# A hybrid decoder block: the merge of the attention groups stores its weights in natural token order and multiplies in halves

## The chip, the cores and the metric

The kernel runs on one core of a Trainium2 chip. The metric is the device time of one execution in microseconds (us), of which several runs are taken and the median is given. The trace is one execution, taken by the hardware profiler.

## What is computed

The block has two branches over 1024 tokens of width 1024: a gated delta rule (8 heads) and a dilated sliding-window attention (4 heads). The change lies in the attention. Each of its heads has three groups with dilations 1, 4 and 16. A group gives, for every token, an unnormalised numerator of 128 channels, the softmax's denominator and the maximum of the row. The groups are then merged by weights that come from the maxima and the denominators:

```
def _dilated_attention(q, k, v):
    ...
    parts = [_dilated_group(q[:, :, i], k[:, :, i], v[:, :, i], win, dil, slopes[i])
             for i, (win, dil) in enumerate(DIL_GROUPS)]
    m_all = parts[0][2]
    for _, _, mx in parts[1:]:
        m_all = jnp.maximum(m_all, mx)
    num = 0.0
    den = 0.0
    for nm, dn, mx in parts:
        sc = jnp.exp(mx - m_all)
        num = num + nm * sc[..., None]
        den = den + dn * sc
    return (num / den[..., None]).reshape(Bn, Sn, DIL_W)
...
        o_b = _dilated_attention(q_b, k_b, v_b) * jax.nn.silu(z_b.astype(f32))
```

## The kernel before

The input projections are done in *units*: two blocks of 128 output columns times 1024 tokens, as a Strassen product of seven products with 12 matmuls each (`gemm_steps`, line 113; the matmuls are line 189). A stationary block is split in two parts, `wh` by ScalarE (line 139) and `wl` by VectorE (line 140), one product ahead of its use; the sums of the stationary blocks are made by GpSimd (lines 152, 153, 165, 166). Results are added from PSUM by VectorE (lines 130, 199, 212).

A head of the attention has five units (`att_unit`, line 753), and its three groups run beside the later ones (`attention`, line 550): scores (line 578), a combined subtraction and minimum on VectorE (line 582), an exponential on ScalarE (line 584), a transpose (line 591), a copy (line 593) and the weighted sum (line 601). A group keeps its tokens in the order (residue, position): group 1 by residues of 4, group 2 by residues of 16. The numerators `num` are `[128 channels, 1024 tokens]` in that order.

The order of TensorE is written out by hand: every generator gets *positions* on a scale in which one unit is 1.0 (`add_stream`, `spread`, and the tables from line 802 on), and `emit` takes the steps in order of position. For the other engines and the DMA queue the Tile scheduler sets the order at build time: of the instructions that its model holds to be ready, the one traced first goes first. Each engine then works strictly in that order. All DMAs are issued from SP, also in order.

`merge` (line 612) is a generator with positions of its own, `MERGE` (line 803), counted from the first unit of its head. At 6.07 the statistics of the three groups are transposed, stored to scratch memory and loaded as `[64, 16]` tiles with 16 tokens to a partition; at 6.52 the weights are worked out (lines 634 to 644) and stored to scratch `w_d`, each group in its own order; from 7.104 on they are loaded broadcast to 128 partitions, multiplied into the numerators (line 654), and the numerators are summed (line 658). The natural order of the tokens comes with these sums: the first group's numerator is viewed with steps of 4 and 16 elements. The last step multiplies by the gate `zs` and stores the head's output.

```
        w_d = dr.tile([3, S], F32, name="w_d", tag="w_d", bufs=2)
        nc.sync.dma_start(w_d[0].rearrange("(l r) -> l r", r=16), cm[:, 0, 0])
        nc.sync.dma_start(w_d[1].rearrange("(r l s) -> l r s", r=4, s=4),
                          cm[:, 0, 1].rearrange("p (r s) -> p r s", s=4))
        nc.sync.dma_start(w_d[2].rearrange("(r l) -> l r", r=16), cm[:, 0, 2])
        yield
        for g in range(3):
            wb = ap_.tile([128, S], F32, name="wb", bufs=2)
            nc.sync.dma_start(wb, w_d[g:g + 1, :].to_broadcast([128, S]))
            V.tensor_tensor(nums[g], nums[g], wb, OP.mult)
            yield
```

The rows of the three stores are 64 B (line 646), 16 B (line 647) and 4 B (line 649) long. After a head's merge the next head's first group runs beside the same unit; after the last head (positions 22 and on) the convolutions of the delta rule (line 904) and its preparation (transposes in line 948) follow. The buffers of the delta rule are taken from the memory of the attention's pool, tile by tile as that comes free.

Of the kernel before, what the change touches and what calls it, by code (L numbers as in the profile page):

```python
# [9 lines left out]
F32 = mybir.dt.float32  # L10
F32R = mybir.dt.float32r
AF = mybir.ActivationFunctionType
OP = mybir.AluOpType
# [3 lines left out]
S = 1024  # L17
# [14 lines left out]
def hybrid_block(ctx: ExitStack, tc: tile.TileContext, x, norm_w, w_in, conv_w, a_log, dt_bias,  # L32
# [27 lines left out]
    @contextmanager  # L60
    def band(level):
        """Instructions traced inside come before all of a higher level when both are ready."""
        saved = tc.cur_priority
        tc.cur_priority = marks.get(level, level * 1000000)
        yield
        marks[level] = tc.cur_priority
        tc.cur_priority = saved

    @contextmanager
    def later(n):  # L70
        """As if traced n instructions later."""
        saved = tc.cur_priority
        tc.cur_priority = saved + n
        yield
        tc.cur_priority = saved
# [24 lines left out]
    ORDER = (("a", "A11", "B11"), ("b", "S2", "T2"), ("a", "A12", "B21"), ("b", "S3", "T3"),  # L100
             ("c", "S1", "T1"), ("b", "A22", "T4"), ("c", "S4", "B22"))
    # the same where the sums of the stationary blocks come late
    ORDER_LATE = (ORDER[0], ("o", "A12", "B21")) + (ORDER[1],) + ORDER[3:]
    # and those of the moving blocks too
    ORDER_LEAD = (ORDER[0], ORDER[2]) + (ORDER[4], ORDER[1], ORDER[3]) + ORDER[5:]

    last_add = [None]
# [5 lines left out]
    def gemm_steps(ops, raw, nk, dest, after, mid=None, late=False, third=None, ahead=0, lead=None):  # L113
        """raw(cb, khalf) -> [128, kh, 128] float32 of column block cb (overwritten).
        dest(cb, half) -> (output AP, view of a [128, 512] result with the output's shape);
        the view of block 0 is the identity or that of block 1. mid() may add to the
        incomplete result of block 1, half 0. With ahead the stationary blocks are made ready one
        product ahead, and the steps end after every three products of one contraction block; lead (with a
        tile for T2, gets a function for the first stationary sum): the sums of either operand come late."""
# [12 lines left out]
        def split(v, first=False):  # L132
# [7 lines left out]
            i = eng.tensor_tensor(wl[:, :kh], v, wh[:, :kh].bitcast(F32), OP.subtract)  # L140
            if third and seen["b"] == 1:
                with tc.issue_after(i.ins):
                    third()
# [86 lines left out]
    def w_raw(w2d, c0, c1, nk, get=raw_tile, which=((0, 0), (1, 1), (1, 0), (0, 1)), tl=None):  # L230
        """Load the two column blocks; 2-D weight [K, N]."""
# [21 lines left out]
    # per head, [p, f] by chunk: exp(-|gc[f] - gc[p]|), and the same with zeros where f < p  # L253
# [5 lines left out]
    # raw weights of the first two units: what is used first beside the first half of the tokens  # L259
# [27 lines left out]
    # norm_w on all partitions  # L287
# [6 lines left out]
    # Moving operands of the Strassen products: sums of the normed rows (quarters of a tile of 128 tokens and  # L294
    # its partner 512 tokens on), transposed on chip and split in two float32r parts.
# [59 lines left out]
    def lead_stream(units):  # L355
        """The first two units; either half of the tokens as it comes."""
# [5 lines left out]
        # S3's slots hold the first stationary blocks  # L362
# [7 lines left out]
        def product(u, n=None):  # L370
            """The next product of unit u; beside it the operand n."""
            for i in range(4):
                next(g[u])
                if n:
                    for j in COLS[i]:
                        part_of_rows(n, j)
                yield
# [46 lines left out]
    # convolution weights and the inner norm's, by channel  # L424
# [6 lines left out]
    def beta_decay():  # L431
        # b and a: the two float32r parts of the 16 columns side by side as one stationary block;
        # second half of the tokens: A21 W0 + A22 W1 = S1 W0 + A22 (W1 - W0)
# [43 lines left out]
        # log1p(e) = ln(u) + (e - (u - 1)) / u, u = 1 + e  # L477
# [40 lines left out]
    def perm(g, ap):  # L518
        """View of [128, n] natural tokens in the group's order (residue, position)."""
# [3 lines left out]
    def proj_unit(b0, b1):  # L523
        """b = (column, dest(half) -> (out AP, psum view), after(half))."""
# [25 lines left out]
    def attention(g, hh, t, st, nums):  # L550
        """Three steps for each block of 128 queries, after two for the values."""
# [60 lines left out]
    def merge(hh, st, nums, t):  # L612
# [8 lines left out]
        # partition = token // 16; the second group's 16 residues are kept in the order (r, s) of 4 s + r  # L621
# [8 lines left out]
        def nat(v, g):  # L630
            """[64, 16] in the order (s, r)."""
# [10 lines left out]
        V.reciprocal(nm, nm)  # L642
        for g in range(3):
            V.tensor_tensor(nat(cm[:, 0, g], g), nat(nm, 0), nat(cm[:, 0, g], g), OP.mult)
        w_d = dr.tile([3, S], F32, name="w_d", tag="w_d", bufs=2)
        nc.sync.dma_start(w_d[0].rearrange("(l r) -> l r", r=16), cm[:, 0, 0])
        nc.sync.dma_start(w_d[1].rearrange("(r l s) -> l r s", r=4, s=4),
                          cm[:, 0, 1].rearrange("p (r s) -> p r s", s=4))
        nc.sync.dma_start(w_d[2].rearrange("(r l) -> l r", r=16), cm[:, 0, 2])
        yield  # L650
        for g in range(3):
            wb = ap_.tile([128, S], F32, name="wb", bufs=2)
            nc.sync.dma_start(wb, w_d[g:g + 1, :].to_broadcast([128, S]))
            V.tensor_tensor(nums[g], nums[g], wb, OP.mult)
            yield
        for g in (1, 2):
            d = DIL[g][1]
            V.tensor_tensor(nums[0].rearrange("p (l r) -> p r l", r=d),  # L658
                            nums[0].rearrange("p (l r) -> p r l", r=d),
                            nums[g].rearrange("p (r l) -> p r l", r=d), OP.add)  # L660
            yield
        V.tensor_tensor(zs[:, :S], zs[:, :S], nums[0], OP.mult)
        nc.sync.dma_start(oB_d[hh], zs[:, :S])
# [3 lines left out]
    def decays(h):  # L667
        """The decay matrices of a head of the gated delta rule, two chunks at a time."""
# [69 lines left out]
    def ya_pair(i):  # L738
        """Two blocks of the first branch's projection, times their gates."""
# [13 lines left out]
    def att_unit(hh, t, pair):  # L753
        """Units of a head, in order: q and k of the first group, v of the first and q of the second,
        k and v of the second, q and k of the third, z and v of the third."""
# [17 lines left out]
    def unit_stream(units):  # L773
        """28 steps each; the weights of the next unit are loaded and made ready beside one. A unit: the two
        blocks (column, dest(half) -> (out AP, psum view), after(half)), the weights, the moving operands."""
# [22 lines left out]
    # The order of the tensor engine, by positions: one unit of the projections in a step.  # L798
    # FIRST: the unit beside which the first convolutions of the gated delta rule run; step n of it has the
    # preparation of half n and the recurrence of half n - 1. RAW, SUMS: sub-steps of a unit. GATES: the gate  # L800
    # units before the end of the rule.
    ATT00, ATT0, ATT1, ATT2 = (2.2, 3.13), (2.139, 3.1), (3.042, 4.541), (5.111, 5.892)
    MERGE, DECAY = (6.07, 6.52, 7.104, 7.12, 7.372, 7.42, 7.584, 7.672, 7.72), (2.417, 2.2)
# [47 lines left out]
    # distances for the two banded groups (previous tile | own tile) and for the 2 x 64 blocks  # L851
# [12 lines left out]
    # rows of the second block do not see the keys of the first  # L864
# [13 lines left out]
    dn = ExitStack()  # L878
    dnp = dn.enter_context(tc.tile_pool(name="dn", bufs=1, reuse_waits="tile"))
    # wmask[j, m] = 1 where j lies in the first block of m's pair of blocks of 16  # L880
# [7 lines left out]
    # one matrix per chunk; a step of 2064 leads from one diagonal block to the next, over chunks too  # L888
# [23 lines left out]
    def scaled(e, o, i, col):  # L912
        """o[p, c, :] = i[p, c, :] * col[p, c]"""
# [6 lines left out]
    def dn_conv(h, hf, t, o):  # L920
        """After either tap of the three convolutions."""
# [7 lines left out]
    def dn_prep(h, hf, o):  # L929
# [59 lines left out]
        # inverse of I + am: 16 x 16 blocks by substitution, then doubled  # L989
# [18 lines left out]
    def dn_run(h, hf, o, state):  # L1008
# [9 lines left out]
        def second(m, b):  # L1018
            """Columns of the second block of each pair of blocks of b."""
# [21 lines left out]
        # blocks of 32: two pairs, 0 and 1, 2 and 3  # L1041
# [18 lines left out]
        # the last doubling acts on one block of 64 x 64  # L1060
# [12 lines left out]
        # recurrence over the four chunks  # L1073
# [64 lines left out]
    def steps(positions):  # L1138
        """Positions of the gated delta rule's steps on the scale of units: the first step takes two."""
# [16 lines left out]
    fin = ctx.enter_context(tc.tile_pool(name="fin", bufs=1, reuse_waits="tile"))  # L1156
    # either half of the contraction, [token block, contraction block, token]
# [5 lines left out]
    def stage(lo, hi, ops_d, kb):  # L1163
        """The sums of the Strassen operands for contraction blocks kb and kb + 4, after the loads."""
# [21 lines left out]
    def split_block(t, tags, eng=V):  # L1186
        """[128, 1024] as two float32r parts."""
# [7 lines left out]
    def sources(n, src, ops_d, t):  # L1195
        """The half t of operand n of a Strassen product; src(contraction block, column half)."""
# [4 lines left out]
    def operand(n, ops, place, tile_of, srcs_of, eng=lambda t: V):  # L1201
        """Operand n into its slots; srcs_of(n, t) None: tile_of(n, t) is loaded."""
# [18 lines left out]
    # the operands used first wait where the sum of the branches comes later  # L1221
# [6 lines left out]
    def stage_a(kb):  # L1228
        """The sums of the first branch's operands for contraction blocks kb and kb + 4, after the loads."""
# [15 lines left out]
    def operand_steps(n):  # L1245
        """Operand n of the projection of the first branch: the loads if it is not there, then its two halves."""
# [196 lines left out]
```

## Time and profile before

| | us |
|---|---|
| median of 3 runs | 1505.6 |
| lowest and highest run | 1503.93, 1506.83 |
| span of the profiled execution, first to last instruction | 1503.7 |
| TensorE busy | 1402.2 (93%) |
| VectorE busy | 1061.7 (71%) |
| ScalarE busy | 728.3 (48%) |
| GpSimd busy | 417.2 (28%) |

The profiled execution's own time is its span; what lies around the span is not in the trace, and the median of the runs is 1.9 us above it. In the rows PE is TensorE, PEld its weight loads, DVE VectorE, ACT ScalarE, POOL GpSimd and SPq the queue on which SP issues DMAs. A matmul's duration reaches past the start of the next one, since matmuls are pipelined: the distance of the starts is what counts. "Idle before" is the time for which the engine had nothing to do, with what ended it.

### The profile page before, as it was taken

To read this page: it belongs to the slowest core of one execution; us is meant where nothing else is said; L and a number is where in the kernel's file an instruction comes from. 1 tells how busy PE (TensorE), PEld (TensorE's weight loads), DVE (VectorE), ACT (ScalarE), POOL (GpSimd) and SP (SyncE) were. 2 spreads that over 40 slices of the span, in tenths; PEclk is the share of its full clock that TensorE was granted. 3 is DMA by queue.
4 is the path that set the end of the run, shared out by engine and by line. 5 is a ranking of instruction groups with operands and counts; after the bars stand their busy time and mean duration, and the time that the engine had idled before them with its cause. 6 is when DMAs were issued, how large, how long until landed. Compare 5 with 4: busy or idle time off the path is not lost.

```text
span 1503.7 us, 22552 instructions
## 1 busy us (share of the span) xinstructions
PE 1402.2 (93%) x7627; PEld 1129.0 (75%) x7627; DVE 1061.7 (71%) x2271; ACT 728.3 (48%) x1828; POOL 417.2 (28%) x398
## 2 busy tenths in 40 slices
PE   7999979997997999799999999999999999999897
PEld 4788868876886887577777777777777787787676
DVE  7765556556556554887877878788877558969876
ACT  5344424433442443565565655556566435424333
POOL 7122312222232222332222223222322222230343
PEclk9999999998998999899999999999999999999999
DMA  6012343233233222642333433343434349679421
GB/s 192 15 51 71 88 76 95 67 89 106 69 90 82 88 64 48 198 117 80 94 109 89 121 101 109 88 108 96 122 94 122 102 132 300 226 238 340 150 106 63
DMA packets 230968, 172.84 MB, mean 115 GB/s; under 512 B 53282, under 2 KB 195011, under 8 KB 230852
## 3 DMA queue, kind: packets, MB, share of 16 engines
q1 hardware_dynamic: 230852, 171.40, 38.8%
q8 instruction: 60, 0.98, 0.3%
q14 instruction: 56, 0.46, 0.1%
HBM read 127.10 MB, written 44.25 MB: 114 GB/s over the span
## 4 chain that ended last, share of the span: by engine, by line
PE 61%; DVE 23%; DMA 7%; ACT 4%; issue 4%; POOL 1%; SPq 0%; POOLq 0%; DVEq 0%; ACTq 0%
PE p_gb L189 19%; PE p_gc L189 13%; PE p_ga L189 12%; DVE wl L140 3%; DVE tp L999 3%; DVE xb L1001 3%; DVE vT L904 2%; PE p_o L601 2%; PE p_ch L578 2%; DMA raw<-in_w_in_dram 2%; DVE qk L904 2%; DMA wb<-w_d 1%; DVE d L130 1%; PE p_w L591 1%; DVE num L658 1%
## 5 line engine op out<-in xcount | busy, mean ns | idle before, releaser
L139 ACT ACTIVATE wh<-raw 128x512 fp32r<-128x512 f32 x283 | 177.7, 629 | 366.1 <-PE p_gc L189 127.2
L140 DVE TENSOR_TENSOR wl<-raw,wh 128x512 fp32r<-128x512 f32 x283 | 206.1, 729 | 37.9 <-PE p_ga L189 15.7
L152 POOL TENSOR_TENSOR raw<-raw 128x512 f32<-128x512 f32 x47 | 64.4, 1370 | 269.0 <-DMA raw<-in_w_in_dram 88.6
L165 POOL TENSOR_TENSOR raw<-raw,t 128x512 f32<-128x512 f32 x46 | 65.7, 1428 | 231.0 <-DVE wl L140 195.2
L166 POOL TENSOR_TENSOR raw<-raw,t 128x512 f32<-128x512 f32 x46 | 61.3, 1332 | 182.2 <-DVE wl L140 174.0
L130 DVE TENSOR_TENSOR d<-p_gc,d 128x512 f32<-128x512 f32 x86 | 59.0, 686 | 50.1 <-PE p_gc L189 50.0
L189 PE MATMUL p_ga<-A11H,wl 128*128 128x512 f32 x184 | 60.2, 430 | 31.7 <-DVE wl L140 31.7
L189 PE MATMUL p_gc<-S4H,wh 128*128 128x512 f32 x204 | 82.2, 405 | 4.3 <-DVE d L130 4.3
L189 PE MATMUL p_gb<-A22H,wh 128*128 128x512 f32 x204 | 83.5, 412 | 2.8 <-DVE d L199 2.8
L189 PE MATMUL p_ga<-A12H,wh 128*128 128x512 f32 x200 | 83.6, 418 | 2.0 <-ACT d L196 1.5
L189 PE MATMUL p_gb<-S3H,wh 128*128 128x512 f32 x188 | 78.8, 422 | 4.7 <-DVE d L199 3.0
L584 ACT ACTIVATE sm<-sm,st 128x128 f32<-128x128 f32 (+1 forms) x96 | 43.1, 449 | 81.7 <-DVE st L582 81.5
L189 PE MATMUL p_gb<-A22L,wh 128*128 128x512 f32 x204 | 81.1, 399 | 0.0
L189 PE MATMUL p_ga<-A12L,wh 128*128 128x512 f32 x200 | 81.0, 405 | 0.0
L189 PE MATMUL p_gb<-S2H,wh 128*128 128x512 f32 x188 | 80.9, 433 | 0.0
L189 PE MATMUL p_gc<-S4L,wh 128*128 128x512 f32 x204 | 80.6, 398 | 0.0
L189 PE MATMUL p_ga<-A11H,wh 128*128 128x512 f32 x184 | 79.4, 432 | 0.6 <-DVE gl L496 0.6
L189 PE MATMUL p_gc<-S1H,wh 128*128 128x512 f32 x188 | 79.4, 425 | 0.0
L904 DVE SCALAR_TENSOR_TENSOR qk<-d,colp,qk 128x512 f32<-128x512 f32 x96 | 76.9, 817 | 1.0 <-ACT qk L902 0.4
L189 PE MATMUL p_gb<-S2L,wh 128*128 128x512 f32 x188 | 77.7, 415 | 0.0
L189 PE MATMUL p_gb<-S3L,wh 128*128 128x512 f32 x188 | 76.3, 408 | 0.0
L189 PE MATMUL p_gc<-S1L,wh 128*128 128x512 f32 x188 | 75.6, 404 | 0.0
(591 smaller groups left out, 3908.6 us busy)
## 6 DMA issues: line engine op xcount, KB each, us to landing
raw<-in_w_in_dram SPq DMA_DIRECT2D x176, 256.0 KB, 3.0
wb<-w_d SPq DMA_DIRECT2D x12, 512.0 KB, 9.1
dr<-gcr_d SPq DMA_DIRECT2D x32, 128.0 KB, 3.0
dec<-de SPq DMA_DIRECT2D x32, 128.0 KB, 1.8
decq<-dr SPq DMA_DIRECT2D x32, 128.0 KB, 1.7
zsp<-d SPq DMA_DIRECT2D x16, 256.0 KB, 2.0
R<-egcr_d SPq DMA_DIRECT2D x16, 256.0 KB, 3.6
sb<-d SPq DMA_DIRECT2D x16, 256.0 KB, 2.6
```

Of the source, the lines that this page charges most:

```text
L130: last_add[0] = V.tensor_tensor(dst, vw(banks[bank]), dst, OP.add)
L139: A.activation(wh[:, :kh], v, AF.Copy)
L140: i = eng.tensor_tensor(wl[:, :kh], v, wh[:, :kh].bitcast(F32), OP.subtract)
L152: e.tensor_tensor(b12, b22, b12, OP.subtract)
L165: (lead["eng"] if lead else G).tensor_tensor(b11, b22, t2, OP.subtract)
L166: G.tensor_tensor(b21, b21, t2, OP.subtract)
L189: T.matmul(pt, w[:, k], m, start=new and n == 0, stop=n == len(prods) - 1, skip_group_check=not new)
L578: T.matmul(pk[:, :n], q[:, m * 128:(m + 1) * 128], k[:, (m + 1) * 128 - n:(m + 1) * 128], start=True, stop=True)
L584: last_exp[0] = A.activation(sm[:, :n], sm[:, :n], AF.Exp, scale=-1.0, bias=st[:, c_m:c_m + 1], accum_out=st[:, c_d:c_d + 1])
L904: V.scalar_tensor_tensor(dst, vw(u[:, o + tap:o + tap + 512]), cw(tap, blk), dst, OP.mult, OP.add)
L999: V.tensor_tensor(tv, bc(ab[:, j + 1:, j:j + 1], [32, ni, nn]), bc(xb[:, 0, j:j + 1, :nn], [32, ni, nn]), OP.mult)
L1001: V.tensor_tensor(xb[:, 0, j + 1:, :nn], xb[:, 0, j + 1:, :nn], tv, OP.subtract)
```

## The change

The weights are written to a new tile `wn` in natural token order, and stored by one DMA with rows of 16 tokens (64 B). The broadcast loads have 512 tokens each and four buffers; four of the six are issued with the store, the last two after the first half's gate product. The order of the groups is now taken care of in the product: the broadcast weights are viewed with steps of 4 or 16 elements, overwritten by the product, and then summed without steps. All six operations of a half are tied behind the last split traced (`issue_after`: on their engine they come after it). The positions are later and more, 14 instead of 9, the last at 7.96 instead of 7.72; so the attention part of the trace ends 0.24 of a unit later as well (`emit(5 * (AH - 1) + max(MERGE) + 0.001)`). Elsewhere the diff takes out comments and docstrings only, which is left out here.

```diff
-    last_add = [None]
+    last_add, last_split = [None], [None]
...
             i = eng.tensor_tensor(wl[:, :kh], v, wh[:, :kh].bitcast(F32), OP.subtract)
+            if not first:
+                last_split[0] = i
...
         V.reciprocal(nm, nm)
+
+        wn = ap_.tile([64, 3, 16], F32, name="wn", bufs=1)
         for g in range(3):
-            V.tensor_tensor(nat(cm[:, 0, g], g), nat(nm, 0), nat(cm[:, 0, g], g), OP.mult)
+            V.tensor_tensor(nat(wn[:, g], 0), nat(nm, 0), nat(cm[:, 0, g], g), OP.mult)
         w_d = dr.tile([3, S], F32, name="w_d", tag="w_d", bufs=2)
-        nc.sync.dma_start(w_d[0].rearrange("(l r) -> l r", r=16), cm[:, 0, 0])
-        nc.sync.dma_start(w_d[1].rearrange("(r l s) -> l r s", r=4, s=4),
-                          cm[:, 0, 1].rearrange("p (r s) -> p r s", s=4))
-        nc.sync.dma_start(w_d[2].rearrange("(r l) -> l r", r=16), cm[:, 0, 2])
-        yield
-        for g in range(3):
-            wb = ap_.tile([128, S], F32, name="wb", bufs=2)
-            nc.sync.dma_start(wb, w_d[g:g + 1, :].to_broadcast([128, S]))
-            V.tensor_tensor(nums[g], nums[g], wb, OP.mult)
+        nc.sync.dma_start(w_d.rearrange("g (l r) -> l g r", r=16), wn)
+
+        def weight(g, hf):
+
+            wb = ap_.tile([128, 512], F32, name="wb", bufs=4)
+            nc.sync.dma_start(wb, w_d[g:g + 1, hf * 512:(hf + 1) * 512].to_broadcast([128, 512]))
+            return wb
+
+        wbs = [[weight(g, hf) for g in range(3 - 2 * hf)] for hf in range(2)]
+        yield
+        for hf in range(2):
+            acc = wbs[hf][0]
+            for g in range(3):
+                wb, num = wbs[hf][g], nums[g]
+                d = DIL[g][1]
+                v = perm(g, wb)
+                o = num[:, hf * 512:(hf + 1) * 512] if d == 1 else num.rearrange("p (r l) -> p r l", r=d)[
+                    :, :, hf * 512 // d:(hf + 1) * 512 // d]
+                with tc.issue_after(last_split[0].ins):
+                    V.tensor_tensor(v, o, v, OP.mult)
+                yield
+                if g:
+                    with tc.issue_after(last_split[0].ins):
+                        V.tensor_tensor(acc, acc, wb, OP.add)
+                    yield
+            z = zs[:, hf * 512:(hf + 1) * 512]
+            with tc.issue_after(last_split[0].ins):
+                V.tensor_tensor(z, z, acc, OP.mult)
+            nc.sync.dma_start(oB_d[hh][:, hf * 512:(hf + 1) * 512], z)
+            if not hf:
+                wbs[1] += [weight(g, 1) for g in (1, 2)]
             yield
-        for g in (1, 2):
-            d = DIL[g][1]
-            V.tensor_tensor(nums[0].rearrange("p (l r) -> p r l", r=d),
-                            nums[0].rearrange("p (l r) -> p r l", r=d),
-                            nums[g].rearrange("p (r l) -> p r l", r=d), OP.add)
-            yield
-        V.tensor_tensor(zs[:, :S], zs[:, :S], nums[0], OP.mult)
-        nc.sync.dma_start(oB_d[hh], zs[:, :S])
...
-    MERGE, DECAY = (6.07, 6.52, 7.104, 7.12, 7.372, 7.42, 7.584, 7.672, 7.72), (2.417, 2.2)
+    MERGE = (6.07, 6.52, 7.3, 7.36, 7.4, 7.46, 7.5, 7.54, 7.7, 7.8, 7.84, 7.88, 7.92, 7.96)
+    DECAY = (2.417, 2.2)
```

## Rows read from the trace of the kernel before

**Rows 1.** The page, part 1: busy time, share of the span and instructions by engine.

```profile
PE 1402.2 (93%) x7627; PEld 1129.0 (75%) x7627; DVE 1061.7 (71%) x2271; ACT 728.3 (48%) x1828; POOL 417.2 (28%) x398
```

**Rows 2.** TensorE's waits, 150 to 640 us: total us, times, longest.

```profile
PE p_ga L189 <- DVE wl L140: 30.8, 4, 8.4
PE p_w L591 <- ACT sm L584: 3.7, 6, 1.2
PE p_gb L189 <- DVE d L199: 2.4, 1, 2.4
```

**Rows 3.** VectorE's waits in the same stretch, the longest of them.

```profile
DVE num L654 <- DMA wb<-w_d: 44.2, 4, 11.8
```

**Rows 4.** VectorE's timeline, first merge: start, us, what [idle before it <- releaser].

```profile
200.52 0.68 DVE L140 TENSOR_TENSOR wl<-raw,wh 128x512 fp32r<-128x512 f32 x1
212.21 1.23 DVE L654 TENSOR_TENSOR num<-num,wb 128x1024 f32<-128x1024 f32 x1 [11.02 <-DMA wb<-w_d]
...
213.96 0.68 DVE L140 TENSOR_TENSOR wl<-raw,wh 128x512 fp32r<-128x512 f32 x1
```

**Rows 5.** SP's timeline, first merge: stores of the weights and first broadcasts.

```profile
196.44 0.50 SPq L646 DMA_DIRECT2D w_d<-cm  x1
197.03 0.60 SPq L647 DMA_DIRECT2D w_d<-cm  x1
197.72 0.57 SPq L649 DMA_DIRECT2D w_d<-cm  x1
198.35 1.82 SPq L653 DMA_DIRECT2D wb<-w_d  x2
```

**Rows 6.** Issue to landing of lines 646, 647, 649 and 653, in this order.

```profile
DMA to landing us min/median/max: 1.8/2.1/2.4
...
DMA to landing us min/median/max: 2.6/3.3/6.2
...
DMA to landing us min/median/max: 9.5/10.6/11.8
...
DMA to landing us min/median/max: 3.5/9.1/14.2
```

**Rows 7.** The page, part 6: another broadcast, 256 KB: times, size, median to landing.

```profile
R<-egcr_d SPq DMA_DIRECT2D x16, 256.0 KB, 3.6
```

**Rows 8.** Busy time by stretch after the four stalls: the last stretch, the sum.

```profile
605.00:611.00 6.00, 4.83 (x12) 3.67 (x12) 5.97 (x6) 0.18 (x1) 2.13 (x1) 0.54 0.32 122
sum 22.00, PE 18.75 PEld 15.13 DVE 21.86 ACT 3.87 POOL 8.52; mean PE 4.69 PEld 3.78 DVE 5.47 ACT 0.97 POOL 2.13
```

The columns of such a row are the stretch, its length, and the busy time with the number of instructions of PE, PEld, DVE, ACT and POOL, then TensorE's granted clock, the share of the DMA engines, and GB/s. The four stretches are 214 to 218, 345 to 351, 475 to 481 and 605 to 611 us.

**Rows 9.** Busy time in a unit with attention and no merge.

```profile
230.00:256.00 26.00, 26.00 (x143) 21.91 (x142) 15.06 (x38) 11.05 (x31) 6.51 (x7) 1.00 0.33 94
```

**Rows 10.** Groups on VectorE, 150 to 640 us: count | busy us, mean ns | idle before.

```profile
L658 DVE TENSOR_TENSOR num<-num 128x1024 f32<-128x1024 f32 x8 | 21.5, 2684 | 0.1
L130 DVE TENSOR_TENSOR d<-p_gc,d 128x512 f32<-128x512 f32 x24 | 16.5, 688 | 13.0 <-PE p_gc L189 13.0
L654 DVE TENSOR_TENSOR num<-num,wb 128x1024 f32<-128x1024 f32 x12 | 14.6, 1220 | 44.2 <-DMA wb<-w_d 44.2
...
L662 DVE TENSOR_TENSOR av<-av,num 128x1024 f32<-128x1024 f32 x4 | 5.9, 1464 | 0.0
```

**Rows 11.** Busy time by stretch, last head: the stall, and what follows it.

```profile
592.40:603.70 11.30, 5.96 (x27) 4.60 (x25) 0.04 (x2) 1.68 (x3) 0.00 (x0) 0.85 0.35 106
603.70:630.10 26.40, 19.90 (x74) 14.82 (x74) 24.46 (x26) 12.59 (x19) 10.05 (x12) 0.87 0.58 189
```

**Rows 12.** TensorE's timeline: starts of the units at two merges, stall, first transposes.

```profile
205.15 0.39 PE L189 MATMUL p_ga<-A11H,wh 128*128 128x512 f32 x1
205.37 0.39 PE L189 MATMUL p_ga<-A11L,wh 128*128 128x512 f32 x1
...
596.39 0.39 PE L189 MATMUL p_ga<-A11H,wh 128*128 128x512 f32 x1
...
606.17 2.08 PE L189 MATMUL p_ga<-A11H,wl 128*128 128x512 f32 x4 [7.81 <-DVE wl L140]
...
630.09 0.66 PE L948 MATMUL p_w<-ident,qk 128*128 128x128 f32 x4 [0.72 <-ACT qk L906]
```

## The prediction, made before the changed kernel ran

> **What bounds the kernel now.** I read the page first: TensorE is busy for 1402.2 of 1503.7 us [rows 1], so it is the bound nearly everywhere, and what can be won is its idle time and the time it runs at half clock. Then the waits of TensorE in the attention part: one wait stands out, four times on `wl`, VectorE's second half of a weight split, 30.8 us together [rows 2]. VectorE's own waits say why `wl` is late: the first product of the merge, `num<-num,wb`, stands for its broadcast of the weights, 44.2 us in four times, once per head [rows 3]. In the timeline of the first merge the reader sees VectorE finish a split at 201.2 us, do nothing until 212.21, multiply, and only then make the split that TensorE is waiting for [rows 4]. VectorE works in order, so a wait for a DMA there becomes a wait of TensorE.
>
> Why the broadcast is late is in the DMA rows. The three stores of the weights are issued between 196.4 and 198.3 us, the first broadcasts right behind them on the same queue [rows 5]. The store of 64 rows of 64 B (line 646) lands in 2.1 us, that of 256 pieces of 16 B (line 647) in 3.3, that of 1024 pieces of 4 B (line 649) in 10.6; the broadcasts behind them land in 3.5 to 14.2, with 9.1 in the middle [rows 6]. I read the 4-byte store as what holds the others up: the fastest 512 KB broadcast needs 3.5 us, so the rest of 14.2 is not its own transfer.
>
> **What the stalls cost.** In the first three heads TensorE stands 30.8 - 7.8 = 23.0 us for `wl` [rows 2, 12], and 3.7 us for the exponentials behind VectorE's backlog [rows 2]. After every stall it runs at half clock: four stretches with a granted clock of 0.50 to 0.54 hold 18.75 us of matmul work, 4.83 of them in the last head [rows 8]. That is the lower of the two levels, 1.2 GHz, after 7 to 8 us without a matmul; at full clock this work takes half, so (18.75 - 4.83)/2 = 7.0 us are lost in the first three heads and 2.4 in the last. First three heads: 23.0 + 3.7 + 7.0 = 33.7 us. Last head: 7.8 + 2.4 (its wait for `d`, [rows 2]) + 2.4 = 12.6. Together 46.3 us, 3% of the span.
>
> **The change, part by part.**
>
> The stores. Three DMAs become one with 192 rows of 64 B. It lies between 64 rows (2.1 us) and 256 pieces (3.3 us) [rows 6]; by the number of pieces I take 2.9. Its cost from both sides: 1.8, the best of line 646, and 10.6, if 64 B behaved like 4 B; the row nearest to it is line 646, which has the same row length. SP issues one instruction instead of three, about 1.2 us less [rows 5]. All of it lies beside TensorE's products, which need none of it.
>
> The loads. Six broadcasts of 256 KB replace three of 512 KB. Four go out right behind the store, since `wb` now has four half buffers; before, the third waited for the first product. A 256 KB broadcast takes 3.6 us [rows 7], a 512 KB one at best 3.5 [rows 6], so halves are not cheaper each. First store issued at 196.5, landed by 199.5, four issues of some 0.4 to 0.9 us, landed by about 205.
>
> The multiplications. They move from 0.1 to 0.3 of a unit's length into the next unit and are tied behind the last split traced. That unit begins at 205.15 us [rows 12] and with attention lasts about 26 us, so the first product is due at about 211 to 213, some 6 to 8 us after its data. So I cost the wait at nothing; what hides it is those 6 us of other VectorE work, and even a store of 10.6 us (196.5 + 10.6 + 3.6 = 211) would barely show. The tie means that the split for the product after next has been issued before VectorE can stand for a broadcast.
>
> VectorE's work. Before: 3 x 1.22 + 2 x 2.68 + 1.46 = 10.5 us per head [rows 10]. After, per half: one product, two sums and the gate product at 0.69 each (a 128x512 operation, line 130 in [rows 10]) and two products with strided views at 2.68/2 plus some 0.06 = 1.4; twice that is 11.1 us. The strided operand has moved from the sum to the product, and its price with it. So VectorE gains nothing: +0.6 us per head.
>
> Where it lies. A unit with attention leaves VectorE 26.00 - 15.06 = 10.9 us free [rows 9]. The twelve operations stand between 0.3 and 0.96 of the unit, 17 us, in which 0.42 x 17 = 7.2 us are free: a backlog of 11.1 - 7.2 = 3.9 us at the end. TensorE has some slack: splits are made one product ahead (12 matmuls of 0.227 us in [rows 12] are 2.7 us), and scores come four steps before their transposes. What exceeds 2.5 us or so stalls it. I take 2 us per head for the first three; bounds 0 (all within the slack) and 5 (the backlog in full and a repeat). The nearest row is the 3.7 us of three heads after the old stalls, 1.2 each [rows 2], when the same work came in one lump.
>
> The last head has no attention behind it but the first convolutions of the delta rule, and VectorE is the bound there: from 603.7 us to the first transposes of the delta rule at 630.09 it is busy for 24.46 of 26.40 us, after 11.3 us with 0.04 [rows 11, 12]. TensorE's unit began at 596.39 [rows 12]; without attention it lasts 84 x 0.227 = 19 us, so the merge may start at 0.3 of it, 602.1. By then VectorE will have done splits and sums for about 3.4 us of the 24.46 (three of 0.68 and two of 0.69). It reaches the same point at 602.1 + 24.5 + 0.6 - 3.4 = 623.8 instead of 630.1: 6.3 us gained, of the 12.6. Bounds: 0, if the merge's later end (0.96 instead of 0.72) moves the convolutions back, since their buffers lie where the merge's were, and 12.6.
>
> The halves' last two loads and the first half's store now stand on SP behind the first half's gate product. Queued behind them are raw weights of the next unit and the decay stores; those weights are needed only at the end of the unit, over 9 us later, so I cost this at nothing, and name it as a rival below.
>
> **The sum.** 33.7 - 3 x 2 + 6.3 = 34.0 us off a span of 1503.7, so 1469.7. The median of the runs is 1505.6, 1.9 above that span, which I carry over: 1505.6 - 34.0 = 1471.6.
>
> **The rivals.**
> 1. *Everything comes back*: the merge hides within the slack in all four heads. 1505.6 - 46.3 = 1459.3. For it: VectorE has 10.9 us free in a unit and needs 11.1. Against: it needs them in two thirds of the unit, and VectorE is the bound after the last head.
> 2. *VectorE becomes the bound*: the backlog of 3.9 us stalls TensorE for 5 us in each of three heads and the last gains nothing: 33.7 - 15 = 18.7, so 1486.9. For it: single operations of 1.4 us between scores and exponentials. Against: the old lump, which held operations of 3 us, cost 1.2 per head.
> 3. *The wait comes back in another place* (slower). The second half's two loads are issued only when the first half's gate product, due at 0.54 plus a backlog of up to 2.9 us, lets go of SP. Their product is due at 0.80, 0.26 x 26 = 6.7 us after 0.54. If they land as late as the old ones, 14.2 us [rows 6], VectorE stands 14.2 - (6.7 - 2.9) = 10.4 us, about the old 11; TensorE loses what it loses now and 2 us per head for the backlog on top: 1505.6 + 8 = 1513.6. It decides from landings of more than about 6 us. Against: the 4-byte store that stood before those loads is gone, and 256 KB takes 3.6 us without it [rows 7]. The Trainium skill, DMA: Bandwidth & Descriptors, section Rules for kernel authors, speaks for this rival, since it asks to coalesce small transfers into large ones, and this change cuts three into six. By that rule the time would go towards this rival's 1513.6; the rows of 3.5 and 3.6 us agree that a half costs as much as a whole [rows 6, 7], but not that it is on the path.
> 4. *It does not do what it says*: the scheduler still places products where VectorE waits. With the tie this needs data later than 211 us; with even the slowest store it would wait some 3 us, within the slack, and the time stays near my forecast.
>
> **How the numbers follow.** My forecast (with rival 4, which gives the same time) 0.57, rival 1 0.17, rival 2 0.16, rival 3 0.06; 0.04 for something between that leaves the time as it is. The likeliest gives 1471.6. The range takes in rivals 1 and 2 with 1 to 3 us for their ends, 1456 to 1488. A measurement of this kernel tells about 0.2% (3 us) from no change: faster 0.91, same 0.03, slower 0.06.
>
> **What would show it.** Right: no idle time of VectorE before the products with `wb`, the wait of TensorE for `wl` gone from the list, full clock through the four stretches, the store landed in 2 to 3.3 us, broadcasts in 3 to 5, VectorE's merge work at about 11 us per head, and a VectorE busy without a break from about 602 us in the last head. Wrong: VectorE idle before the second half's products (rival 3); many waits of TensorE for `st`, `sm` or `wl` of 1 us and more between 0.3 and 1 of a unit (rival 2); a store of 64-byte rows that takes 10 us, or convolutions that begin no earlier than before.

## The result, and the profile after

The changed kernel took 1464.85 us (median of 4 runs, 1462.11 to 1465.42), the kernel before 1504.76 beside it (4 runs, 1502.91 to 1506.83). The ratio is 0.9725, with a 95% interval of 0.9711 to 0.9739: faster by 2.75%. The profiled execution's span is 1462.7 us instead of 1503.7. The page's part 1 has TensorE busy for 8.8 us less than in [rows 1], in a span 41.0 us shorter:

```profile
PE 1393.4 (95%) x7627; PEld 1123.9 (77%) x7627; DVE 1065.7 (73%) x2295; ACT 728.9 (50%) x1828; POOL 416.4 (28%) x398
```

Where the 41.0 us came from can be read off two marks. The transposes of the statistics (one group per head, line 615 before, 617 after) open each merge, and the first transposes of the delta rule close the attention part [rows 12]. Before, by tile `st`, first and last start:

```profile
L615 PE MATMUL p_w<-ident,st x4: 270/270/270, 187.3 to 578.6; 128*48 128x128 f32 x4
```

After, the same view:

```profile
L617 PE MATMUL p_w<-ident,st x4: 270/270/270, 186.4 to 544.1; 128*48 128x128 f32 x4
```

After, TensorE's timeline at the second mark (start, us, what, idle before it and its releaser):

```profile
589.41 1.11 PE L967 MATMUL p_w<-ident,qk 128*128 128x128 f32 x4 [7.37 <-ACT qk L925]
```

From the first group of transposes to the fourth, three heads took 391.3 us before and take 357.7: 33.6 us less. From the fourth to the first product of the delta rule the last head took 630.09 - 578.6 = 51.5 and takes 45.3: 6.2 less. The rest of the program gives 1.2. In the last head TensorE still stands, 7.37 us in front of the delta rule's first transposes where the kernel before stood 7.81 for `wl` [rows 12]: there the stall has moved, and only part of the time came back.

TensorE's waits from 150 to 640 us (total, times, longest), where [rows 2] had 30.8 us for `wl` and 3.7 for `sm`:

```profile
PE p_w L967 <- ACT qk L925: 7.4, 1, 7.4
PE p_gb L191 <- DVE d L214: 2.8, 2, 1.4
PE p_o L603 <- DVE pT L595: 0.6, 3, 0.2
```

All three heads together wait 0.6 us; the other two rows lie in the last head. Busy time from the first to the fourth group of transposes, before and after (columns as in [rows 8]):

```profile
187.30:578.60 391.30, 364.64 (x1796) 301.19 (x1795) 226.66 (x493) 153.78 (x366) 97.87 (x91) 0.97 0.32 82
186.40:544.10 357.70, 357.10 (x1795) 296.04 (x1794) 230.76 (x511) 153.56 (x366) 100.38 (x91) 1.00 0.33 89
```

So of the 33.6 us, 26.1 are idle time of TensorE (391.30 - 364.64 = 26.7 before, 0.6 after) and 7.5 are busy time. The granted clock is 1.00 over the three heads, so the half-clock stretches of [rows 8] are gone there.

SP's timeline at the first merge, against [rows 5]: one store, four broadcasts behind it, the other two singly, 18 and 22 us later.

```profile
195.98 0.60 SPq L650 DMA_DIRECT2D w_d<-wn  x1
197.88 1.77 SPq L655 DMA_DIRECT2D wb<-w_d  x4
...
215.87 0.32 SPq L655 DMA_DIRECT2D wb<-w_d  x1
...
220.26 0.32 SPq L655 DMA_DIRECT2D wb<-w_d  x1
221.19 0.32 SPq L678 DMA_DIRECT2D oB<-av  x1
```

The page's list of DMA issues has the median from issue to landing of the broadcasts, against 9.1 us in [rows 6]; the store's was 1.9 us:

```profile
wb<-w_d SPq DMA_DIRECT2D x24, 256.0 KB, 4.1
```

VectorE's timeline at the first merge, against [rows 4]. No merge operation (lines 669 to 677) has an idle time in front of it, and between them stand the attention's score operations (`sm`, `st`), copies (`pT`) and splits (`wl`):

```profile
212.86 0.68 DVE L669 TENSOR_TENSOR wb<-num,wb 128x512 f32<-128x512 f32 x1
213.46 0.42 DVE L584 CUSTOM_DVE_ANT_0 sm<-p_ch,bias 128x256 f32<-128x256 f32 x1
213.81 0.08 DVE L584 DVE_READ_ACCUMULATOR2_ANT st<- 128x1 f32 x1
213.81 1.11 DVE L669 TENSOR_TENSOR wb<-num,wb 128x512 f32<-128x512 f32 x1
214.81 0.42 DVE L595 COPY pT<-p_w 128x256 f32<-128x256 f32 x1
215.15 0.69 DVE L673 TENSOR_TENSOR wb<-wb 128x512 f32<-128x512 f32 x1
215.75 0.69 DVE L140 TENSOR_TENSOR wl<-raw,wh 128x512 fp32r<-128x512 f32 x1
216.35 2.17 DVE L669 TENSOR_TENSOR wb<-num,wb 128x512 f32<-128x512 f32 x1
```

The backlog that the prediction feared is there: busy time by stretch shows VectorE (third of the engines) busy for 19.73 of 20 us. TensorE (first) is busy for 19.81 of them:

```profile
216.00:226.00 10.00, 10.00 (x55) 8.48 (x54) 10.00 (x19) 3.85 (x11) 3.60 (x3) 1.00 0.55 147
226.00:236.00 10.00, 9.81 (x57) 7.72 (x56) 9.73 (x19) 3.49 (x10) 2.99 (x4) 1.00 0.37 117
```

In the last head VectorE is the bound, as predicted. From 0.3 of its unit, which begins at 561.94 us, to the first transposes of the delta rule it is busy for 21.64 of 21.81 us, TensorE for 13.11:

```profile
567.60:589.41 21.81, 13.11 (x58) 10.25 (x56) 21.64 (x28) 11.60 (x18) 6.74 (x11) 0.90 0.57 173
```

### The profile page after: what moved, and what is told of

It is laid out like the page before. It is cut to its first block, busy times and chain, and to the rows that moved or that the text cites. A ratio compares the mean times of both kernels' runs of the same rounds, so it can differ in the third digit from the quotient of the medians.

```text
span 1462.7 us, 22580 instructions
## 1 busy us (share of the span) xinstructions
PE 1393.4 (95%) x7627; PEld 1123.9 (77%) x7627; DVE 1065.7 (73%) x2295; ACT 728.9 (50%) x1828; POOL 416.4 (28%) x398
## 4 chain that ended last, share of the span: by engine, by line
PE 67%; DVE 22%; ACT 4%; issue 3%; DMA 2%; POOL 1%; SPq 0%; POOLq 0%; DVEq 0%; ACTq 0%
PE p_gb L191 21%; PE p_gc L191 15%; PE p_ga L191 14%; DVE wl L140 3%; DVE tp L1018 3%; DVE vT L923 2%; DVE xb L1020 2%; PE p_o L603 2%; PE p_ch L580 2%; DVE qk L923 2%; PE p_ch L1047 1%; PE p_w L984 1%; DVE d L201 1%; PE p_w L593 1%; DVE d L130 1%
## 5 line engine op out<-in xcount | busy, mean ns | idle before, releaser
L167 POOL TENSOR_TENSOR raw<-raw,t 128x512 f32<-128x512 f32 x46 | 61.8, 1344 | 195.0 <-DVE wl L140 176.8
L168 POOL TENSOR_TENSOR raw<-raw,t 128x512 f32<-128x512 f32 x46 | 59.2, 1286 | 172.6 <-DVE wl L140 164.1
L191 PE MATMUL p_ga<-A11L,wh 128*128 128x512 f32 x184 | 73.2, 398 | 0.0
```

Of the source, the lines that this page charges most:

```text
L167: (lead["eng"] if lead else G).tensor_tensor(b11, b22, t2, OP.subtract)
L168: G.tensor_tensor(b21, b21, t2, OP.subtract)
L191: T.matmul(pt, w[:, k], m, start=new and n == 0, stop=n == len(prods) - 1, skip_group_check=not new)
```

## The experiments

The change has four separable parts: the quick store, the tie behind the last split, the later place, and halves with four buffers and unstepped sums. The kernels below turn them on and off; the slow store is the three old ones in e2, and one of 4-byte pieces more in e1 and e7. The whole rows of e4 and e8 are summed without steps too, since the new store's order allows it. Each ratio is to the kernel before, run beside it. "Heads 1-3" and "head 4" are the two distances of the section above, in us, from each kernel's own profile.

| kernel | store | tied, placed | operations | ratio to before [95%] | heads 1-3 | head 4 |
|---|---|---|---|---|---|---|
| before | slow | no, early | whole | 1 | 391.3 | 51.5 |
| e7 | slow | no, late | halves | 0.9967 [0.9953, 0.9981] | 389.6 | 51.3 |
| e2 | slow | yes, late | whole | 0.982 [0.9805, 0.9834] | 368.1 | 51.6 |
| e1 | slow | yes, late | halves | 0.9741 [0.9718, 0.9764] | 356.9 | 52.0 |
| e3 | quick | no, late | halves | 0.9801 [0.9783, 0.982] | 372.8 | 41.2 |
| e4 | quick | no, early | whole | 0.9754 [0.9739, 0.9769] | 367.5 | 41.1 |
| e8 | quick | yes, late | whole | 0.9749 [0.9732, 0.9765] | 362.3 | 45.5 |
| changed | quick | yes, late | halves | 0.9725 [0.9711, 0.9739] | 357.7 | 45.3 |
| e6 | quick | yes, early | halves | 0.971 [0.9696, 0.9725] | 359.2 | 42.8 |
| e5 | quick | yes, last head early | halves | 0.9705 [0.969, 0.9719] | 357.5 | 42.0 |

**The slow store put back (e1).** A store of 4-byte pieces, which nothing reads, goes in front of the new store:

```diff
+        x_d = dr.tile([S], F32, name="x_d", tag="x_d", bufs=2)
+        nc.sync.dma_start(x_d.rearrange("(r l) -> l r", r=16), wn[:, 2])
         nc.sync.dma_start(w_d.rearrange("g (l r) -> l g r", r=16), wn)
```

> The changed kernel with a store of 1024 pieces of 4 B, read by nobody, put back in front of the new store on SP. Theory (the order of VectorE decides, the store hardly): the new store or the broadcasts behind it land about 8 to 10 us later than in the changed kernel (1.9 and 4.1 us there), the first product with wb, which started at 212.9 us there with 6 us and more in hand, waits at most 3 us, TensorE does not stand for wl, and the time stays within 1461 to 1470 us. Rival (the 4-byte store is the cause and its removal the cure): VectorE stands 7 to 11 us per head for wb again and the time goes to 1490 or more.

Measured: 1468.97 us. SP's timeline of e1 shows that the delay is real: the broadcasts leave 10 us later than in the changed kernel, since the new store behind the slow one lands 9.7 us after its issue.

```profile
195.98 0.61 SPq L651 DMA_DIRECT2D x_d<-wn  x1
196.64 0.67 SPq L652 DMA_DIRECT2D w_d<-wn  x1
198.13 0.37 SPq L239 DMA_DIRECT2D raw<-in_w_in_dram  x1
208.35 1.77 SPq L657 DMA_DIRECT2D wb<-w_d  x4
```

Yet the first three heads take 356.9 us, as in the changed kernel: tied and late, a slow store is hidden entirely. Only the last head pays, and elsewhere: the broadcasts stand on SP in front of a load of the gates (`zsp`), and VectorE and then TensorE wait for that one. VectorE's waits of e1:

```profile
DVE d L201 <- DMA zsp<-d: 8.8, 1, 8.8
```

TensorE's:

```profile
PE p_gb L191 <- DVE d L201: 4.9, 1, 4.9
```

**The tie taken out (e3).** `with tc.issue_after(last_split[0].ins):` goes from the products, the sums and the gate products; places and store stay.

> The changed kernel without the tie behind the last split, store and positions as changed; VectorE's order then has the first products in front of the split that the next product of TensorE needs, where they stood before the change. Theory: with the quick store the broadcasts land near 202 us, so VectorE stands 2 to 4 us per head, TensorE 0 to 1.5 us, and the time is 1463 to 1473 us. Rival (the tie is the cure by itself): VectorE stands as before, 10 us and more, and the time is above 1490 us.

Measured: 1478.4 us, above what I expected and under the rival's. VectorE's waits for the broadcasts are small (6.7 us in six, less than the 2 to 4 per head that I expected). The lump is not: with no tie the pieces come as soon as there is data. VectorE's timeline of e3 (lines left out within) has the first product at 199.65 us, and the scores, on which the next exponentials hang, only at 211.82 (TensorE's product for them ended at 207.4; in the changed kernel VectorE took it at 209.57, as soon as it ended):

```profile
199.65 1.70 DVE L668 TENSOR_TENSOR wb<-num,wb 128x512 f32<-128x512 f32 x2 [1.48 <-DMA wb<-w_d]
...
210.50 1.40 DVE L671 TENSOR_TENSOR wb<-wb 128x512 f32<-128x512 f32 x1
211.82 0.28 DVE L584 CUSTOM_DVE_ANT_0 sm<-p_ch,bias 128x128 f32<-128x128 f32 x1
```

TensorE's waits of e3:

```profile
PE p_w L593 <- ACT sm L586: 10.2, 3, 3.7
```

So the tie is worth 15 us in three heads, by keeping the merge out of the way of the next group's start: the 10.2 us of waits, and 5.5 us more of TensorE's busy time (362.57 us instead of 357.10, at a granted clock of 0.98 over these heads). In the last head, where no attention follows, the same haste gains 4 us.

**Both put back (e7).** The slow store of e1 in the kernel of e3.

> Both undone: the 4-byte store in front and no tie. Theory (either cure alone is enough, so only without both does the stall return): VectorE stands 8 to 12 us per head for wb, TensorE 6 to 9 us per head for wl with half clock after it, and the time is 1490 to 1508 us. Rival (the gain came from the halves, the four buffers or the sums without steps): the time stays below 1475 us.

Measured: 1503.94 us, and the stall of before is back nearly whole (30.8 and 44.2 us there [rows 2, 3]). TensorE's waits of e7:

```profile
PE p_ga L191 <- DVE wl L140: 27.7, 4, 7.4
```

VectorE's:

```profile
DVE wb L670 <- DMA wb<-w_d: 41.7, 4, 11.2
```

Halves, four buffers, unstepped sums and late places by themselves bring 0.3%. The old stall needs two things at once, late data and a product put in front of a split; either cure takes it away (the tie in e1, the store in e3; the later place alone does not, since e7 has it).

**The tie alone, on the kernel before (e2).** Its stores, whole broadcasts and two buffers, with the tie and later places:

```diff
-    MERGE, DECAY = (6.07, 6.52, 7.104, 7.12, 7.372, 7.42, 7.584, 7.672, 7.72), (2.417, 2.2)
+    MERGE, DECAY = (6.07, 6.52, 7.3, 7.36, 7.46, 7.52, 7.6, 7.68, 7.72), (2.417, 2.2)
...
-            V.tensor_tensor(nums[g], nums[g], wb, OP.mult)
+            with tc.issue_after(last_split[0].ins):
+                V.tensor_tensor(nums[g], nums[g], wb, OP.mult)
```

> The kernel before with its three stores, whole broadcasts and two buffers, but the products and sums tied behind the last split and moved to 7.3 to 7.68. Theory: the slow store is hidden behind the 11 to 12 us between the store and the first product, VectorE stands 0 to 3 us per head, and the time is 1463 to 1475 us. Rival (the quick store is needed): TensorE stands 5 us and more per head and the time is above 1485 us.

Measured: 1481.6 us, between the two expectations. VectorE waits only 4.6 us for broadcasts that land in up to 17.6. What is left over the changed kernel is 10.4 us in three heads, in which TensorE waits 7.4 us for copies (`pT`) and 1.5 for numerators, and 6.3 in the last. The last head's is e1's again (the same 8.8 us for `zsp`, 4.9 on TensorE).

**The store alone, on the kernel before (e4).** Early, untied, whole rows:

```diff
-        nc.sync.dma_start(w_d[0].rearrange("(l r) -> l r", r=16), cm[:, 0, 0])
...
+        nc.sync.dma_start(w_d.rearrange("g (l r) -> l g r", r=16), wn)
...
+                V.tensor_tensor(perm(g, wb), nums[g].rearrange("p (r l) -> p r l", r=d), perm(g, wb), OP.mult)
...
+            V.tensor_tensor(nums[0], nums[0], wbs[g], OP.add)
```

> Only the store is changed against the kernel before: the weights are multiplied into a tile in natural order and leave by one store of 64-byte rows; the places of the steps, the whole rows (two buffers), and the lack of a tie stay as before, and so the second and third product are written with strides over the broadcast tile. My theory (a quick store lets the broadcasts land some 10 us earlier, and an early product stands at most a few us; what is left is that the products go in a lump before the first stationary part and the first exps): VectorE waits 2 to 7 us in a head for the broadcasts, the ratio to the kernel before is 0.978 to 0.988 (1472 to 1488 us). Rival 1 (the tie is the cure, the store hardly matters): over 0.993, VectorE stands for the broadcasts by over 30 us in all, as before. Rival 2 (the store is all): at or below 0.974, as the changed kernel.

Measured: 1467.61 us, a little below the range I gave, clear of the first rival and just short of the second. VectorE's waits of e4:

```profile
DVE num L656 <- DMA wb<-w_d: 9.4, 4, 3.1
```

TensorE's:

```profile
PE p_w L591 <- ACT sm L584: 7.9, 3, 3.1
```

2.4 us per head of standing for the data are within TensorE's slack, the lump costs 7.9 us of waits in three heads, and the last head does best of all (41.1). The store alone is about nine tenths of the change: 2.46 of 2.75%.

**Store and tie, whole rows (e8).** The kernel of e4 with e2's places and ties.

> The kernel with the old store and whole rows, tied and late (0.982), but with the quick store, and products written with strides over the broadcast tile so that the sums are unstepped: it stands between that kernel and the changed one, from which it differs by whole rows and two buffers alone. My theory (with tie and late place the store hardly matters; whole operations of 1.2 to 2.8 us and the third broadcast, which waits for a buffer, cost the rest): VectorE's wait for a broadcast is under 5 us, ratio 0.977 to 0.982. Rival (it was the slow store after all that cost the 10 us): 0.972 to 0.975, as the changed kernel.

Measured: 1467.55 us, below my range and at the upper end of the rival's: the rival was right. The store, with the unstepped sums that its order allows, was worth 5.8 us in three heads and 6.1 in the last on top of e2's tie. What halves add to it is small. TensorE's waits of e8 have one row that the changed kernel has at 0.6 us:

```profile
PE p_o L603 <- DVE pT L595: 4.7, 3, 1.7
```

These are copies that come late, where whole operations of some 2 us stand in the queue. The 4.1 us between them are most of the difference of the heads, 362.3 - 357.7 = 4.6; of the two ratios the intervals overlap.

**Early places with the tie (e6).** One line: `MERGE = (6.07, 6.52, 7.104, 7.12, 7.14, 7.16, 7.18, 7.2, 7.372, 7.42, 7.48, 7.584, 7.672, 7.72)`.

> The changed kernel with its merge steps about where the kernel before had them (first half 7.104 to 7.2, second half 7.372 to 7.72), the tie kept. My theory (with the tie the products cannot come before the last stationary part of the unit's operands is split, so that the place in the order matters little, except that the last head begins its convolutions earlier): no wait of VectorE for a broadcast, no wait of TensorE for wl over 3 us in all, the ratio to the kernel before is 0.968 to 0.974. Rival (the later place itself is what avoids the lump in front of the first exps): TensorE waits 5 to 10 us for exps (sm) over the heads, as without the tie, and the ratio is 0.977 to 0.982.

Measured: 1461.1 us, within my range, with no wait for a broadcast. Waits for exponentials are 2.6 us in three (10.2 without the tie): the tie, not the later place, is what keeps the lump away. The last head gains 2.5 us.

**The last head earlier (e5, e10), the changed kernel beside it (e9), and without its tie (e11).**

```diff
+    MERGE_LAST = (6.07, 6.52, 7.02, 7.06, 7.1, 7.14, 7.18, 7.22, 7.35, 7.4, 7.44, 7.48, 7.52, 7.56)
...
-        add_stream(m, [5 * hh + p for p in MERGE])
+        add_stream(m, [5 * hh + p for p in (MERGE if hh < AH - 1 else MERGE_LAST)])
...
-    emit(5 * (AH - 1) + max(MERGE) + 0.001)
+    emit(5 * (AH - 1) + max(MERGE_LAST) + 0.001)
```

> The changed kernel, but for the last head, where the merge's steps from the second barrier on are placed 0.28 to 0.4 of a unit earlier (7.02 to 7.56 in place of 7.3 to 7.96). My theory (in the last head the merge's and the convolutions' work on VectorE is what TensorE waits for at the first convolution product, 7.4 us, while VectorE has idle gaps of 1.4 to 2 us beside the head's last projection unit before the merge begins): that wait falls to 1 to 4 us, and the ratio to the kernel before is 0.968 to 0.971 (4 to 7 us below the changed kernel). Rival (VectorE's work between the head's last sums and the convolutions is what counts, wherever the steps stand): no change, 0.972 to 0.974. Other rival (the earlier products go ahead of exps and stationary parts of the last unit, so that TensorE waits there by as much): 0.974 or more, with waits for wl or sm of over 5 us.

Measured: 1460.76 us. TensorE's waits of e5, where the changed kernel had 7.4 us for the convolutions:

```profile
PE p_gb L191 <- DVE d L214: 3.2, 2, 2.7
PE p_w L968 <- ACT qk L926: 2.4, 1, 2.4
PE p_gb L191 <- DVE d L201: 1.9, 1, 1.9
```

A gain this small was asked again, beside the changed kernel on one chip:

> The changed kernel as it is, beside the kernel with its last head's merge earlier on the same chip: ratio to the kernel before 0.971 to 0.974. If the earlier last head is a real gain, this one lies 3 to 5 us above it; if the difference of the runs before came from the chip, the two agree within 1.5 us.

> The kernel whose last head has its merge steps 0.28 to 0.4 of a unit earlier, once more: ratio to the kernel before 0.969 to 0.972, and 3 to 5 us below the changed kernel on this chip (rival: within 1.5 us of it).

> The same early last head, and its products and sums no longer tied behind the last split (heads 1 to 3 keep the tie). The stretch from the last head's transposes of the statistics to the first convolution product took 42.0 us with the tie; without a tie two other kernels had 41.1 and 41.2. My theory (in the last head nothing but VectorE's order of work counts; a tie holds a product back by a us at most): 0 to 1.5 us below the one with the tie, which cannot be told from no change. Rival (without the tie a product stands for its broadcast in front of the last stationary parts, and the 3 us come back as waits for wl): 2 to 4 us above it.

Measured: the changed kernel 1465.12 us, 0.9725 [0.9711, 0.974]; the earlier last head 1461.21, 0.9702 [0.9684, 0.9719]; without its tie 1460.55, 0.9704 [0.9686, 0.9722]. The earlier last head is 3.9 us better by the medians, 4.1 in the first comparison; both times the intervals still overlap a little, so that it is likely and not certain. Where it lies differs between the two profiles: the last head took 42.0 us in e5 and 43.6 in e10, against 45.3 in both profiles of the changed kernel, and in e10 more of the gain lies behind the head, where the changed kernel runs its first 10 us at a granted clock of 0.71 and e10 at 1.00. Taking out the tie made no difference that can be seen.

## Why the prediction held, and where it was off

- **The stall and its cause** (late data because of the 4-byte store, a product in front of a split): shown by e7 against e1 and e3. What I had not seen is that either cure is enough; I had argued it for the tie and the later place alone ("even a store of 10.6 us [...] would barely show"), and e1 bears that out for the three heads.
- **What the stalls cost**: 33.7 us in the first three heads as read; 33.6 came back. The two parts hold as well: 26.7 us of waits read and 26.1 back, 7.0 us of half clock read and 7.5 back, with the clock at 1.00. That the whole came back to 0.1 us is in part luck, since 0.6 us of waits are left and the half clock was read 0.5 too small.
- **The store**: 1.9 us to land where I took 2.9, close to my lower bound of 1.8. The trace agrees that 64-byte rows behave like line 646.
- **The wait costed at nothing**: right. VectorE never waits for `wb`; e1 shows the cover, e4 what it costs if the cover is gone (2.4 us per head on VectorE).
- **The term that was mis-sized: "I take 2 us per head for the first three"**, the backlog's price, 6 us of the sum. It measured 0.6 us in all. The backlog came (VectorE busy for 19.73 of 20 us, with more merge work than forecast), so what was mis-sized is TensorE's slack against it. I had treated the backlog as one delay for everything on VectorE. In the timeline it falls on the merge's own pieces: a score, a copy or a split stands behind one piece. e8 supports this, since with whole operations TensorE waits 4.7 us for copies.
- **VectorE's work**: 11.1 us per head forecast. By the groups of the changed kernel it is (26.0 + 17.4 + 6.4)/4 = 12.5 (last section).
- **The last head**: 6.3 us forecast, 6.2 measured. The reason I gave is that VectorE has 24.5 + 0.6 - 3.4 = 21.7 us of work from 0.3 of the unit to the first transposes. The row of that stretch has 21.64 us of VectorE in 21.81. e5 and e10 support it too, where beginning earlier gave 3.3 and 1.7 us more in this head.
- **The rivals.** The first (everything comes back) is what happened in three heads, not in the last. The second and the third did not happen: broadcasts landed in 3.4 to 5.2 us. The Trainium skill, DMA: Bandwidth & Descriptors, section Rules for kernel authors, asks to coalesce small transfers; here loads of half the size left the time no worse (e8 against the changed kernel), since no engine waited for one.
- **The sum**: 1471.6 forecast, 1464.85 measured. Of the 6.8 us, 5.9 lie in the first three heads (33.6 against 27.7): 5.4 are the backlog's, 0.6 us in place of 6.0, and 0.5 the half clock's. Another 0.8 is the level of these runs of before (1504.76 against 1505.6).

## What to carry to other kernels

When an engine stands for a DMA, look at both sides: what makes the data late (here a store in 4-byte pieces ahead on the same queue) and what stands behind the waiting instruction; mending either removes the stall, and a store in longer rows is the smaller edit. Background work on an in-order engine did little harm here once it was cut into pieces shorter than the slack of what waits behind each piece (0.6 us of waits in three heads; 4.7 with pieces of some 2 us), and tied so that it can't go ahead of the next stage's first steps (10.2 us without the tie). Place it anew where the surroundings change: in the last head, with nothing to hide under, an earlier place was better by some 4 us, by the medians.

## What was not expected of the hardware

The same VectorE operation has two durations. By group (count, busy us, mean ns, idle before) of the changed kernel:

```profile
L669 DVE TENSOR_TENSOR wb<-num,wb 128x512 f32<-128x512 f32 x24 | 26.0, 1088 | 0.0
L673 DVE TENSOR_TENSOR wb<-wb 128x512 f32<-128x512 f32 x16 | 17.4, 1086 | 0.1
L677 DVE TENSOR_TENSOR av<-av,wb 128x512 f32<-128x512 f32 x8 | 6.4, 799 | 0.0
```

An unstepped sum (line 673) takes 0.69 us in the median and up to 1.74; a product with steps takes 1.09 and up to 2.19. VectorE's timeline in the last head:

```profile
570.57 0.69 DVE L673 TENSOR_TENSOR wb<-wb 128x512 f32<-128x512 f32 x1
...
571.78 1.10 DVE L669 TENSOR_TENSOR wb<-num,wb 128x512 f32<-128x512 f32 x1
572.91 1.67 DVE L673 TENSOR_TENSOR wb<-wb 128x512 f32<-128x512 f32 x1
574.61 1.67 DVE L677 TENSOR_TENSOR av<-av,wb 128x512 f32<-128x512 f32 x1
```

GpSimd's, the same stretch:

```profile
572.04 1.99 POOL L154 TENSOR_TENSOR raw<-raw 128x512 f32<-128x512 f32 x1 [5.07 <-DVE wl L140]
574.11 1.62 POOL L155 TENSOR_TENSOR t<-raw 128x512 f32<-128x512 f32 x1
```

The two long operations end at 574.58 and 576.28 us, each 0.55 us after a GpSimd operation that ended at 574.03 and 575.73: as if VectorE had stood until GpSimd was done and then run. The timelines show the same of all the long ones: eleven of the 48 merge operations take over 1.2 us, each of them begins while a GpSimd TENSOR_TENSOR runs, and the seven sums and the gate product among them end 0.54 to 0.56 us after it, the three products with steps 0.93 to 0.96. None of the other 37 begins beside such an operation. The Trainium skill, SBUF — State Buffer, section SBUF: two separate sides, states such a rule: a VectorE operation with two SBUF inputs and a GpSimd operation that reads SBUF exclude each other for a whole instruction. These rows agree with it; no kernel here was made to test it. It bears on the term that I sized at 11.1 us: alone, a head's twelve operations would take 2 x (0.68 + 2 x 1.09 + 2 x 0.69 + 0.68) = 9.8 us, and 12.5 were measured. What the eleven take above these times, 10.6 us in four heads, accounts for that difference.

A second one: on SP's queue a quick store behind a slow one lands late. The store of 64-byte rows took 1.9 us by itself and 9.7 behind the 4-byte store of e1, on which it does not depend.
